# Products of the block inverse as 64x64 tiles, and half of the recurrence's matmuls on the array's other diagonal

## The chip, the cores and the metric

The kernel runs on one core of one Trainium2 chip. The metric is the device time of the whole program in microseconds (us), the median of three runs.

## The reference, cut to what matters here

The program is two transformer-like blocks over 512 tokens of width 1024. The change lies in the first block's mixer, an RWKV recurrence of 8 heads of 64 channels, run over 256 context tokens and then 512 tokens, forwards (d = 0) and backwards (d = 1):

```python
def wkv_scan(state0, r, decay, kk, b, v, k, reverse):
    def step(S, inp):
        r_t, w_t, kk_t, b_t, v_t, k_t = inp
        sa = jnp.einsum("bhvk,bhk->bhv", S, kk_t)
        S = (S * w_t[:, :, None, :] - sa[..., None] * b_t[:, :, None, :]
             + v_t[..., None] * k_t[:, :, None, :])
        return S, jnp.einsum("bhvk,bhk->bhv", S, r_t)
    ...
```

The kernel does this chunk by chunk: 12 chunks of 64 tokens in each direction, for a pair of heads at a time. Within a chunk the steps become a triangular system, so for each chunk, direction and head the inverse of a 64x64 unit triangular matrix is wanted.

## The kernel before

The 128 partitions hold two heads of 64; there are four such pairs, j = 0 to 3. `prep(j)` makes a pair's operands and `stage(j)` runs its recurrence. `build` calls `proj` (the projections, and `prep(0)` and most of `prep(1)` within it), then `rwkv`, then `tail` (output projection, FFN and the whole second block).

`prep(j)` is a generator. For each direction d it makes decays and gates (names `sg`, `cs`, `ta`, `b`), the operands `KB` and `KR`, and then the products that the inverse needs (line 633, PSUM tile `pa`, in the tag `mm` with one buffer). A product of two 64-token operands is wanted as four 32x32 blocks: the two on the block diagonal go to `AKD`, the two beside it to `AKO`. Each block is one matmul of 64 rows and 32 columns of the array, so a direction has 12 chunks x 2 blocks x 2 heads = 48 of them for `AKD` and 48 for `AKO`. One ACT copy (line 188) takes each set out of PSUM. `AKD` has one buffer, `AKO` two.

`inverse(j)` then works on both directions at once. DVE transposes `AKD` into `U` (line 662) and inverts all 32x32 diagonal blocks by 31 steps of two DVE operations on `tmp` and `X` (lines 670, 671), and transposes `X` into `F1` and `F2` (lines 673, 674, both `F` in the rows). PE multiplies `AKO` by them in 32x32 tiles (`pt`, line 691), ACT copies (`T`), PE multiplies again (`po`, lines 698 and 699), and ACT writes the last blocks of the result `XT`.

`stage(j)` runs 12 groups g; in each group one chunk of either direction. For two groups at a time, `pair` makes scores (`psc`, masked by DVE into `AS`, line 731) and transposed operands (`pkt`, copied by ACT into `kbt`). A chunk's chain is: residual `pr` (from `AS`, `vt` and from `KR`, the state `S`), ACT copy to `RU`, correction `pu` (`XT` times `RU`), ACT copy, state update `p3` (`kbt`, `RU`), ACT copy to `S`; and an output `py` beside it. `pr`, `pu` and `py` lie in one PSUM bank for each direction, `p3` in another. All these matmuls go through `mmh`: one matmul for each head, rows 64h to 64h+63 of the array into columns 64h to 64h+63. After a stage, `gn(j)` normalises its output (`ys`, `gm`, `yc`, `gv`), the last stage's on the way to the output projection.

A scheduler sets the order of the work on each engine, by priorities: a stage takes 200 for each group, and the steps of `prep` (a step ends at each `yield`) are taken up between, 4 in each group of stage 0, 2 in stage 1. Stages 0 and 1 so carry `prep(2)` and `prep(3)`. The buffers of `prep` are given up when `inverse(3)` is done; their room goes to the weights of what follows, first to the 32 loads `adaw` with one DVE product each (line 540, `ada12`), which run beside stages 2 and 3.

Of the kernel before, what the change touches and what calls it, by code (L numbers as in the profile page):

```python
# [10 lines left out]
F32 = mybir.dt.float32  # L11
# [7 lines left out]
P = 128  # L19
# [103 lines left out]
class K:  # L123
# [120 lines left out]
    def build(self):  # L244
        tc = self.tc
        with ExitStack() as es:
            self.dr = es.enter_context(tc.tile_pool(name="dr", bufs=1, space=bass.MemoryType.DRAM))
            self.ea = es.enter_context(ExitStack())
            p0 = self.p0 = self.pool(es, "p0", side="left")
            self.cst = p0.tile([P, NCST], F32, name="cst")  # L250
            self.vec = p0.tile([P, NVEC], F32, name="vec")
            self.mod = p0.tile([P, 48, 2], F32, name="mod")
            self.scz = p0.tile([P, KD, 32], F32, name="scz")
            self.mhalf = p0.tile([P, 16], F32, name="mhalf")
            zxb = p0.tile([P, KD, NX], F32, name="zx")
            self.zx = [zxb[:, k, :] for k in range(KD)]
            with ExitStack() as er:
                r0 = self.r0 = self.pool(er, "r0", side="left")
                self.sg = r0.tile([P, NX], F32, name="sg")
                self.vD = self.dr.tile([P, 4, 12, 64], F32, name="vD")  # L260
                self.rD, self.kD, self.kkD = [[self.dr.tile([P, n], F32, name=f"{t}D{j}") for j in range(4)] for t, n in (("r", NX), ("k", NT), ("kk", NT))]
                st = lambda p, name, shape: p.tile([P] + shape, F32, name=name)
                XT0, XT1 = self.XT0, _ = st(r0, "XT0", [24, 64]), zxb[:, 5:8, :].rearrange("p a (b c) -> p (a b) c", c=64)
                set0 = {"KB": [st(r0, f"KB0{d}", [12, 2, 64]) for d in range(2)], "KR": [st(r0, f"KR0{d}", [1280]) for d in range(2)]}
                self.sets = [dict(set0, XT=XT0), {"XT": XT1}, None, dict(set0, XT=XT0)]
                self.hb, self.kah = st(r0, "hb", [16]), st(r0, "kah", [4, 4])
                with ExitStack() as ep:
                    self.pp = self.pool(ep, "pp", side="right")
                    self.lin = [self.pp.tile([P, NT], F32R, name=f"lin{i}") for i in range(2)]

                    room = [(f"KB1{d}", 6) for d in range(2)] + [("KR10", 5)]
                    self.room = []
                    for tag, n in room:
                        t = self.pp.tile([P, n, NC_], F32, tag=tag, name="adaw", bufs=1).rearrange("p a b -> p (a b)")
                        self.room += [t[:, i * 512:i * 512 + 512].unsqueeze(1) for i in range(n // 2)]
                    self.psp = self.psum(ep, "psp", side="right")
                    self.AKD = st(self.pp, "AKD", [32, 32])
                    with ExitStack() as e1:
                        self.wp = self.r1 = self.pool(e1, "r1", side="left")
# [19 lines left out]
    def proj(self):  # L299
# [48 lines left out]
        for kc in range(KD):  # L348
# [4 lines left out]
            for i in range(2):  # L353
# [5 lines left out]
                    nc.gpsimd.tensor_tensor(out=hlo[i][kc], in0=xT[i][kc], in1=hhi[i][kc].bitcast(F32), op=ALU.subtract)  # L359
                else:  # L360
                    nc.vector.scalar_tensor_tensor(out=hlo[i][kc], in0=xT[i][kc], scalar=sh, in1=hhi[i][kc].bitcast(F32), op0=ALU.add, op1=ALU.subtract)
        nc.gpsimd.memset(self.AKD, 0.0)

        def tile_of(u, x=True, c=True):
            ws = [ahead.pop((u, k0), None) or piece(u, k0) for k0 in (0, 4)]
# [179 lines left out]
    def prep(self, j):  # L545
# [23 lines left out]
        nc.scalar.activation(out=bo, in_=pb, func=AF.Copy)  # L569
        S["bo"] = bo  # L570
        ch = lambda t: t.rearrange("p (c t) -> p c t", t=64)
        AKO = S["AKO"] = pp.tile([P, 24, 32], F32, tag="AKO", name="AKO", bufs=2)
        for d in range(2):
            def lora(i, out, bias):

# [46 lines left out]
            nc.vector.tensor_tensor(out=krx[:, :, 1, :], in0=ch(rt), in1=inc[:, 4:12, :], op=ALU.mult)  # L622
            yield

            for off, A in enumerate((self.AKD, AKO)):
                pa = psm(384, "pa")
                for c in range(12):
                    kp = krc[:, c, :] if c < 4 else krx[:, c - 4, 0, :]
                    lt, rt_ = (kp, kb[:, c, bs, :]) if d else (kb[:, c, bs, :], kp)
                    for q in range(2):  # L630
                        o, i = 32 * q, 32 * (q ^ off)
                        for h in (0, 64):
                            nc.tensor.matmul(pa[h + o:h + o + 32, c * 32:c * 32 + 32], lt[h:h + 64, o:o + 32], rt_[h:h + 64, i:i + 32], start=True, stop=True)
                    if c == 5:
                        yield
                self.copy(nc.scalar, A[:, 12 * d:12 * d + 12, :], pa.rearrange("p (c t) -> p c t", t=32))
                yield
        yield from self.inverse(j)

    def mmh(self, out, lt, rt, start=True, stop=True):  # L640

        for h in range(2):
            hs = slice(64 * h, 64 * h + 64)
            self.nc.tensor.matmul(out[hs], lt[hs], rt[hs], start=start, stop=stop)

    @contextmanager
    def prio(self, p):
# [6 lines left out]
    def inverse(self, j):  # L654
# [2 lines left out]

        nc, pp = self.nc, self.pp
        big = lambda name: pp.tile([P, 32, 32], F32, tag="inv", name=name, bufs=3)
        XT, AKO = self.S[j]["XT"], self.S[j]["AKO"]  # L660
        U, tmp, X = big("U"), big("tmp").rearrange("p a b -> p (a b)"), big("X")
        nc.vector.transpose(out=U, in_=self.AKD.rearrange("p n i -> p i n"))
        nc.gpsimd.memset(X, 0.0)
        nc.gpsimd.memset(X.rearrange("p a b -> p (a b)")[:, ::33], 1.0)
        for k in range(31):
# [7 lines left out]
        nc.vector.transpose(out=F1.rearrange("p n i -> p i n"), in_=X)  # L673
        nc.vector.transpose(out=F2.rearrange("p n j -> p j n"), in_=X.rearrange("p i j -> p j i"))
        yield
        b0, b1 = [slice(o, o + 32) for o in (0, 64)], [slice(o + 32, o + 64) for o in (0, 64)]
        D = slice(0, 12), slice(12, 24)
        for r, F in zip(D, (F1, F2)):
            self.copy(nc.vector, XT[:, r, :].rearrange("p n (q i) -> p n q i", q=2), F[:, r, :].unsqueeze(2).to_broadcast([P, 12, 2, 32]))
# [6 lines left out]
        for r in D:  # L686
            yield
            pt = ps("pt")
            for n in range(r.start, r.stop):
                for h in range(2):  # L690
                    nc.tensor.matmul(pt[b1[h], n - r.start, :], AKO[b0[h], n, :], F2[b0[h], n, :], start=True, stop=True)
            for h in range(2):
                self.copy(nc.scalar, T[b1[h], r, :], pt[b1[h]])
        yield
# [9 lines left out]
    def stage(self, j, S, todo, rb, gn):  # L704
# [35 lines left out]
        for g in range(12):  # L740
            at = base + self.PK * g
            with self.prio(at):
                if g % 2 == 0:
                    for d in range(2):
                        pair(g // 2, d)
                for d in range(2):
                    c = chunk(d, g)
                    A, kt, KR, x = cells.pop((d, c))
                    V, S0 = vt[:, c, :], self.S0[d]
                    R, U = (self.RU[d][g % 2][:, i, :] for i in range(2))  # L750
                    pr, pu, py = (self.C1[d][:, i * 64:i * 64 + 64] for i in range(3))
                    p3 = self.C2[d][:, 0:64]
                    self.mmh(pr, A[:, 0:64], V, True, g == 0)
                    if g:
                        self.mmh(pr, KR[:, 0:64], S0, False, True)
                    nc.scalar.activation(out=R, in_=pr, func=AF.Copy)
                    if g < 11:
                        self.mmh(p3, kt[:, 0], V, True, False)
                        if g:
                            self.mmh(p3, id2, S0, False, False)  # L760
                    self.mmh(pu, XT[:, 12 * d + c, :], R)
                    nc.scalar.activation(out=U, in_=pu, func=AF.Copy, scale=-1.0)
                    if x:
                        self.mmh(py, A[:, 64:P], V, True, False)
                        self.mmh(py, KR[:, 64:P], S0, False, False)
                    if g < 11:
                        self.mmh(p3, kt[:, 1], U, False, True)
                        nc.scalar.activation(out=S0, in_=p3, func=AF.Copy, scale=S["PC"][d][:, c:c + 1])
                    if x:
                        self.mmh(py, A[:, P:192], U, False, True)  # L770
                        self.copy(nc.scalar, Y[d][:, c - 4, :], py)
            with self.prio(at + self.PG):
                next(gn, None)
# [6 lines left out]
    def gn(self, j, Y, bo, vt):  # L780
# [43 lines left out]
        yield  # L824
        py = self.ps2.tile([P, 8, 64], F32, tag="sc", name="py", bufs=2)
        for i in range(8):
            self.mmh(py[:, i, :], yc[:, i, :], self.c("id2"))
        nc.vector.scalar_tensor_tensor(out=z, in0=py.rearrange("p a b -> p (a b)"), scalar=self.v("lng", j), in1=z, op0=ALU.mult, op1=ALU.add)
        yield
        if j < 3:  # L830
# [564 lines left out]
```

## Time and profile before

| | |
|---|---|
| median of three runs | 1617.11 us (1615.75 to 1618.56) |
| the profiled execution | 1620.11 us, of which its span is 1618.3 us |
| TensorE (PE), busy | 1533.4 us, 95% |
| VectorE (DVE), busy | 998.3 us, 62% |
| ScalarE (ACT), busy | 629.8 us, 39% |
| stages 0 to 3 | from about 260 to 552 us in the span |

Busy time of PE counts a matmul to the end that the profile models for it, so a row of small matmuls that wait for one another's results can still read as busy. The table of 40 slices is in steps of 40.5 us. [...]

### The profile page before, as it was taken

What the parts mean: (1) busy time and instruction counts of PE and PEld (TensorE: products, weight loads), DVE (VectorE), ACT (ScalarE), POOL (GpSimd) and SP (SyncE); (2) the same over time, 40 slices, a digit from 0 to 9 for tenths busy, and PEclk for the clock granted to TensorE, in tenths of its full rate; (3) what the DMA queues carried; (4) which work ended last, traced back from release to release, by engine and by line L of the source; (5) the groups of instructions that cost most, each with busy time, mean ns of one, the idle gap of its engine ahead of it and who ended that gap; (6) DMA issues with size and microseconds to landing.
All of it is one profiled execution on the core that took longest, in us unless ns stands there. A gap on an engine that the chain in (4) does not pass through costs nothing. (4 is left out here: it accounts for less than half of the span.)

```text
span 1618.3 us, 31205 instructions
## 1 busy us (share of the span) xinstructions
PE 1533.4 (95%) x13214; PEld 1254.0 (77%) x13214; DVE 998.3 (62%) x1689; ACT 629.8 (39%) x1258; POOL 116.8 (7%) x133
## 2 busy tenths in 40 slices
PE   4999999899988899999999997999999999999998
PEld 2877777788777699888888885887677888888886
DVE  3447758873577478888883437678965555554221
ACT  3524344454244344333332335334554333333222
POOL 1111000110101000000000004121200000000000
PEclk9999999797689999999999999999999999999999
DMA  9243321100138442323223332211022222323321
GB/s 333 85 155 101 105 85 57 35 13 4 38 108 258 152 142 80 104 91 104 92 89 94 95 101 69 90 56 51 27 66 91 92 91 91 103 93 92 104 82 61
DMA packets 62188, 152.98 MB, mean 95 GB/s; under 512 B 12640, under 2 KB 14432, under 8 KB 62048
## 3 DMA queue, kind: packets, MB, share of 16 engines
q1 hardware_dynamic: 58016, 143.95, 27.6%
q10 hardware_dynamic: 4032, 7.04, 1.3%
q8 instruction: 103, 1.69, 0.4%
q14 instruction: 37, 0.30, 0.1%
HBM read 143.10 MB, written 7.86 MB: 93 GB/s over the span
## 5 line engine op out<-in xcount | busy, mean ns | idle before, releaser
L181 ACT ACTIVATE whi<-w 128x1024 fp32r<-128x1024 f32 (+2 forms) x220 | 209.0, 952 | 453.6 <-PE pm L170 336.2
L182 DVE TENSOR_TENSOR wlo<-w,whi 128x1024 fp32r<-128x1024 f32 (+2 forms) x212 | 229.5, 1084 | 211.5 <-ACT whi L181 206.8
L169 PE MATMUL pm<-ahi,whi 128*128 128x512 f32 (+1 forms) x624 | 236.5, 379 | 2.6 <-DVE sh L1078 2.2
L170 PE MATMUL pm<-alo,whi 128*128 128x512 f32 (+1 forms) x624 | 234.8, 376 | 0.0
L171 PE MATMUL pm<-ahi,wlo 128*128 128x512 f32 (+1 forms) x624 | 234.0, 375 | 0.0
L170 PE MATMUL pm<-al,whi 128*128 128x512 f32 x352 | 139.7, 397 | 0.0
L169 PE MATMUL pm<-ah,whi 128*128 128x512 f32 x352 | 139.2, 395 | 0.0
L171 PE MATMUL pm<-ah,wlo 128*128 128x512 f32 x352 | 139.2, 395 | 0.0
L169 PEld LDWEIGHTS pm<-ahi,whi 128*128 128x128 f32 x624 | 117.6, 188 | 23.9 <-ACT sh L1093 2.6
L171 PEld LDWEIGHTS pm<-ahi,wlo 128*128 128x128 f32 x624 | 117.6, 188 | 20.9 <-issue 0.7
L170 PEld LDWEIGHTS pm<-alo,whi 128*128 128x128 f32 x624 | 117.6, 189 | 20.0 <-issue 0.7
L951 DVE SCALAR_TENSOR_TENSOR cv<-pm,vec,cv 128x441 f32<-128x441 f32 (+2 forms) x176 | 121.1, 693 | 4.1
L171 PEld LDWEIGHTS pm<-ah,wlo 128*128 128x128 f32 x352 | 66.2, 188 | 16.1 <-issue 0.2
L170 PEld LDWEIGHTS pm<-al,whi 128*128 128x128 f32 x352 | 66.2, 188 | 16.1 <-issue 0.2
L169 PEld LDWEIGHTS pm<-ah,whi 128*128 128x128 f32 x352 | 66.2, 188 | 16.0
L169 PE MATMUL pm<-hhi,whi 128*128 128x512 f32 x176 | 71.3, 405 | 0.5 <-ACT whi L181 0.5
L171 PE MATMUL pm<-hhi,wlo 128*128 128x512 f32 x176 | 70.6, 401 | 1.0 <-DVE wlo L182 1.0
L170 PE MATMUL pm<-hlo,whi 128*128 128x512 f32 x176 | 69.9, 397 | 0.0
L169 PE MATMUL pd<-whi,gh 128*128 128x512 f32 x176 | 69.5, 395 | 0.0
L169 PE MATMUL pm<-hh,whi 128*128 128x512 f32 x176 | 69.3, 394 | 0.0
L170 PE MATMUL pm<-hl,whi 128*128 128x512 f32 x176 | 69.3, 394 | 0.0
L171 PE MATMUL pm<-hh,wlo 128*128 128x512 f32 x176 | 69.3, 394 | 0.0
(397 smaller groups left out, 3140.2 us busy)
## 6 DMA issues: line engine op xcount, KB each, us to landing
w<-in_fup SPq DMA_DIRECT2D x44, 512.0 KB, 3.4
adaw<-in_adat SPq DMA_DIRECT2D x32, 512.0 KB, 4.6
w<-in_win SPq DMA_DIRECT2D x44, 256.0 KB, 2.9
w<-in_wg SPq DMA_DIRECT2D x22, 512.0 KB, 3.4
w<-in_wu SPq DMA_DIRECT2D x22, 512.0 KB, 3.4
w<-in_wd SPq DMA_DIRECT2D x22, 512.0 KB, 3.6
w<-in_win SPq DMA_DIRECT2D x18, 512.0 KB, 3.4
w<-in_wout SPq DMA_DIRECT2D x16, 512.0 KB, 3.8
```

Of the source, the lines that this page charges most:

```text
L169: nc.tensor.matmul(out, lh, rh, start=(first and i == 0), stop=False)
L170: nc.tensor.matmul(out, lh, rl, start=False, stop=False)
L171: nc.tensor.matmul(out, ll, rh, start=False, stop=(last and i == n - 1))
L181: self.nc.scalar.activation(out=hi, in_=src, func=AF.Copy)
L182: (eng or self.nc.vector).tensor_tensor(out=lo, in0=src, in1=hi.bitcast(F32), op=ALU.subtract)
L951: nc.vector.scalar_tensor_tensor(out=o, in0=p[:, ro[0] + dr:ro[1] + dr, co[0] + dc:co[1] + dc], scalar=w(i), in1=o, op0=ALU.mult, op1=ALU.add)
```

## The change

The products of the inverse are made as whole 64x64 blocks, one matmul for each chunk and head, in two sets of six chunks for each direction; they land in one tile `AK` of 24 x 64 columns with one buffer, which takes the place of `AKD` and `AKO`. Before the inverse, two GpSimd (POOL) copies bring the second diagonal block beside the first; a `yield` follows them. `mmh` gets a switch, `swap`: head h then goes from rows 64h into the columns of the other head. It is set for `pa`, `pr`, `pu`, `py` and for the transposition of `yc` in `gn`, so that the two heads stand exchanged in `AK`, `XT`, `RU`'s first half and `Y`, and come back into place in the second product. `p3`, `psc`, `pkt` stay as they were.

```diff
-                    self.AKD = st(self.pp, "AKD", [32, 32])
+                    self.AK = st(self.pp, "AK", [32, 64])
...
-        AKO = S["AKO"] = pp.tile([P, 24, 32], F32, tag="AKO", name="AKO", bufs=2)
...
-            for off, A in enumerate((self.AKD, AKO)):
+            for q in range(2):
                 pa = psm(384, "pa")
-                for c in range(12):
+                for c in range(6 * q, 6 * q + 6):
                     kp = krc[:, c, :] if c < 4 else krx[:, c - 4, 0, :]
                     lt, rt_ = (kp, kb[:, c, bs, :]) if d else (kb[:, c, bs, :], kp)
-                    for q in range(2):
-                        o, i = 32 * q, 32 * (q ^ off)
-                        for h in (0, 64):
-                            nc.tensor.matmul(pa[h + o:h + o + 32, c * 32:c * 32 + 32], lt[h:h + 64, o:o + 32], rt_[h:h + 64, i:i + 32], start=True, stop=True)
-                    if c == 5:
-                        yield
-                self.copy(nc.scalar, A[:, 12 * d:12 * d + 12, :], pa.rearrange("p (c t) -> p c t", t=32))
+                    self.mmh(pa[:, (c - 6 * q) * 64:(c - 6 * q) * 64 + 64], lt, rt_, swap=True)
+                n = 12 * d + 6 * q
+                self.copy(nc.scalar, self.AK[:, n:n + 6, :], pa.rearrange("p (c t) -> p c t", t=64))
                 yield
...
-            hs = slice(64 * h, 64 * h + 64)
-            self.nc.tensor.matmul(out[hs], lt[hs], rt[hs], start=start, stop=stop)
+            hs, ho = (slice(64 * i, 64 * i + 64) for i in (h, h ^ swap))
+            self.nc.tensor.matmul(out[ho], lt[hs], rt[hs], start=start, stop=stop)
...
+        for h in range(2):
+            nc.gpsimd.tensor_copy(out=AK[b1[h], 0:24, 0:32], in_=AK[b1[h], 0:24, 32:64])
+        yield
         U, tmp, X = big("U"), big("tmp").rearrange("p a b -> p (a b)"), big("X")
-        nc.vector.transpose(out=U, in_=self.AKD.rearrange("p n i -> p i n"))
+        nc.vector.transpose(out=U, in_=AK[:, :, 0:32].rearrange("p n i -> p i n"))
...
-                    self.mmh(pr, A[:, 0:64], V, True, g == 0)
+                    self.mmh(pr, A[:, 0:64], V, True, g == 0, swap=True)
                     if g:
-                        self.mmh(pr, KR[:, 0:64], S0, False, True)
+                        self.mmh(pr, KR[:, 0:64], S0, False, True, swap=True)
...
-                    self.mmh(pu, XT[:, 12 * d + c, :], R)
+                    self.mmh(pu, XT[:, 12 * d + c, :], R, swap=True)
...
-                        self.mmh(py, A[:, P:192], U, False, True)
+                        self.mmh(py, A[:, P:192], U, False, True, swap=True)
```

What the scheduler makes of it is seen in three places. First PE near the end of stage 1, where the products of `prep(3)`, d = 1, are made. `pkt` and `psc` are the operands and scores of the stage's next two groups, `c` the PSUM tiles of the chain. (The shapes are those of the moving operand; a 32x32 row of `pa` has 64 rows of the array.) Before, where one row stands for the other for some 40 rows:

```order
L644 MATMUL pkt<-cst,KB_1789 64x64
L633 MATMUL pa<-KB_85,KR_87 32x32
L644 MATMUL pkt<-cst,KB_1789 64x64
L633 MATMUL pa<-KB_85,KR_87 32x32
L644 MATMUL pkt<-cst,KB_1789 64x64
L633 MATMUL pa<-KB_85,KR_87 32x32 x2
L644 MATMUL psc<-KR_1792,KB_1790 64x128
L633 MATMUL pa<-KB_85,KR_87 32x32
```

and PE at the same products in the changed kernel, which make up these three rows and none besides:

```order
L639 MATMUL pkt<-cst,KB_2360 64x64 x8
L639 MATMUL pa<-KB_85,KR_87 64x64 x8
L639 MATMUL c_2375<-RU_2369,zx 64x64 x2
L639 MATMUL pa<-KB_85,KR_87 64x64 x4
L639 MATMUL c_2376<-RU_2371,zx 64x64 x2
L639 MATMUL c_2375<-vt,AS_2366 64x64 x2
L639 MATMUL c_2375<-S_2373,KR_1648 64x64 x2
L639 MATMUL c_2377<-RU_2369,kbt 64x64 x2
L639 MATMUL c_2375<-RU_2369,AS_2366 64x64
L639 MATMUL pa<-KB_85,KR_87 64x64 x12
```

The 96 matmuls in single file with the stage's are now 24 in three pieces. From the first score of stage 0 to the end of the recurrence `pa` stands in 74 rows on PE before and in 13 now; the neighbours in PE's row that lie on different diagonals are 479 now and none before. Second, ACT in stage 0, at the end of `inverse(1)`; `T` are its copies, `zx` its results, `AK` (`AKD`, `AKO`) the products of `prep(2)`. Before:

```order
L188 ACTIVATE T<-pt 32x384 x4
L188 ACTIVATE zx<-po 32x12x32 x4
L188 ACTIVATE AKD<-pa 128x384
L188 ACTIVATE kbt<-pkt 128x256
L756 ACTIVATE RU_2633<-c_2639 128x64
```

and ACT at the same end of `inverse(1)` in the changed kernel:

```order
L188 ACTIVATE AK<-pa 128x384
L188 ACTIVATE T<-pt 32x384 x2
L762 ACTIVATE RU_2370<-c_2375 128x64
L188 ACTIVATE T<-pt 32x384 x2
L188 ACTIVATE AK<-pa 128x384
L768 ACTIVATE S_2373<-c_2377,pc 128x64
```

Before, the `AKD` shown is that of d = 1; the products of d = 0 had left PSUM 27 and 26 rows above the first row shown. Now those of d = 0 stand among the copies of `inverse(1)`, since its `pt` still reads `AK`, and what follows in `prep(2)` stands behind them. Third, DVE from the end of `inverse(1)` to the start of `inverse(2)`. Before, where these twelve rows are all there is between:

```order
L673 STREAM_TRANSPOSE F_2869<-X 128x32x32
L674 STREAM_TRANSPOSE F_2870<-X 128x32x32
L192 COPY zx<-F_2869 128x768
L192 COPY zx<-F_2870 128x768
L613 SCALAR_TENSOR_TENSOR KB_2625<-b_3428,sg 128x12x64
L621 TENSOR_TENSOR KR_2627<-kk,cs 128x8x64
L615 TENSOR_TENSOR b_3428<-ta,kt 128x768
L622 TENSOR_TENSOR KR_2627<-rt,cs 128x8x64
L616 TENSOR_TENSOR KB_2625<-b_3428,sg 128x12x64
L731 COPY_PREDICATED AS_2629<-cst,psc 128x384
L731 COPY_PREDICATED AS_2631<-cst,psc 128x384
L662 STREAM_TRANSPOSE U<-AKD 128x1024
```

and DVE from the same place in the changed kernel, where `U` comes three rows after the last one shown:

```order
L192 COPY zx<-F_2520 128x768
L730 COPY_PREDICATED AS_2366<-cst,psc 128x384
L190 TENSOR_SCALAR sg<-sg,cst 128x12x64
L594 SCALAR_TENSOR_TENSOR cs<-cst,sg 128x780
L730 COPY_PREDICATED AS_2368<-cst,psc 128x384
L611 SCALAR_TENSOR_TENSOR b_2983<-ta,kk 128x768
L730 COPY_PREDICATED AS_2365<-cst,psc 128x2x64
L612 SCALAR_TENSOR_TENSOR KB_2361<-b_2983,sg 128x12x64
L619 TENSOR_TENSOR KR_2363<-kk,cs 128x256
L620 TENSOR_TENSOR KR_2363<-kk,cs 128x8x64
L614 TENSOR_TENSOR b_2983<-ta,kt 128x768
L621 TENSOR_TENSOR KR_2363<-rt,cs 128x8x64
```

Now the whole of d = 1 (`sg`, `cs`, `b`, `KB`, `KR`) comes after the end of `inverse(1)`, where before only its last half did. Counted in masks `AS` of the stages (12 in each) ahead of them in DVE's row, the three ends `F` of inverses 1 to 3 stood behind 8, 18 and 30, and stand behind 10, 22 and 32 now.

## Rows read from the trace of the kernel before

**Rows 1.** The page: busy time of the engines, and the granted clock in 40 slices.

```profile
PE 1533.4 (95%) x13214; PEld 1254.0 (77%) x13214; DVE 998.3 (62%) x1689; ACT 629.8 (39%) x1258; POOL 116.8 (7%) x133
...
PEclk9999999797689999999999999999999999999999
```

**Rows 2.** Stretches: us, then busy us (instructions) of PE, PEld, DVE, ACT, POOL, PEclk.

```profile
260.00:300.00 40.00, 37.55 (x977) 31.39 (x968) 34.48 (x82) 21.52 (x75) 0.57 (x2) 1.00 0.03 9
...
380.00:430.00 50.00, 49.33 (x851) 39.63 (x852) 21.13 (x42) 17.16 (x63) 1.51 (x4) 0.74 0.01 4
...
470.00:550.00 80.00, 68.26 (x1611) 59.19 (x1606) 56.94 (x98) 35.19 (x149) 4.90 (x3) 1.00 0.75 240
```

**Rows 3.** Timeline of PE, stage 1: start, us, operation, number of passes merged.

```profile
409.06 0.31 PE L633 MATMUL pa<-KB,KR 64*32 64x32 f32 x2
409.30 0.47 PE L644 MATMUL pkt<-cst,KB 64*64 64x64 f32 x2
409.70 0.31 PE L633 MATMUL pa<-KB,KR 64*32 64x32 f32 x2
```

**Rows 4.** Timeline of PE, stage 1, some 47 us earlier.

```profile
361.95 0.24 PE L633 MATMUL pa<-KR,KB 64*32 64x32 f32 x2
362.12 0.32 PE L644 MATMUL c<-vt,kbt 64*64 64x64 f32 x2
362.38 0.24 PE L633 MATMUL pa<-KR,KB 64*32 64x32 f32 x2
```

**Rows 5.** Timeline of PE, stage 3, matmuls of one tile size alone.

```profile
522.58 0.28 PE L644 MATMUL c<-S,KR 64*64 64x64 f32 x4
522.70 0.28 PE L644 MATMUL c<-RU,kbt 64*64 64x64 f32 x4
```

**Rows 6.** DVE, starts of `U` and `F`: inverses 1 to 3, idle time before in brackets.

```profile
301.77 1.95 DVE L673 STREAM_TRANSPOSE F<-X 128x1024 f32<-128x1024 f32 x1
...
315.45 1.95 DVE L662 STREAM_TRANSPOSE U<-AKD 128x1024 f32<-128x1024 f32 x1 [4.32 <-ACT AKD L188]
...
361.33 1.92 DVE L673 STREAM_TRANSPOSE F<-X 128x1024 f32<-128x1024 f32 x1
...
403.60 1.93 DVE L662 STREAM_TRANSPOSE U<-AKD 128x1024 f32<-128x1024 f32 x1 [8.13 <-ACT AKD L188]
...
451.88 1.95 DVE L673 STREAM_TRANSPOSE F<-X 128x1024 f32<-128x1024 f32 x1
```

**Rows 7.** Waits of DVE, 315.5 to 361.3: us in total, times, longest.

```profile
DVE AS L731 <- PE psc L644: 7.7, 3, 5.3
```

**Rows 8.** The same, 361.4 to 403.7.

```profile
DVE AS L731 <- PE psc L644: 11.7, 2, 11.2
DVE U L662 <- ACT AKD L188: 8.1, 1, 8.1
DVE sg L190 <- ACT sg L580: 3.6, 1, 3.6
```

**Rows 9.** The same, 403.7 to 451.9.

```profile
DVE AS L731 <- PE psc L644: 16.3, 6, 9.2
```

**Rows 10.** POOL's groups by form: a plain copy of 64 partitions x 512.

```profile
L1127 POOL COPY kz<-ak 64x512 f32<-64x512 f32 x4 | 3.5, 878 | 13.7 <-ACT ak L1119 13.6
```

**Rows 11.** Timeline of POOL and DVE: `gn` of stages 2 and 3 begins with `ys`.

```profile
493.17 2.25 POOL L807 TENSOR_TENSOR ys<-Y 128x512 f32<-128x512 f32 x1
...
552.12 1.14 DVE L807 TENSOR_TENSOR ys<-Y 128x512 f32<-128x512 f32 x1 [6.60 <-ACT Y L188]
```

**Rows 12.** Tile `adaw`: durations ns min/median/max, first and last start in us.

```profile
L540 DVE SCALAR_TENSOR_TENSOR adaw<-adaw,cb x32: 1208/1224/1939, 471.3 to 533.8; 128x1024 f32<-128x1024 f32 x32
```

**Rows 13.** Timeline, PE and its weight loads (PEld), `po` of `inverse(0)`.

```profile
189.66 0.21 PE L698 MATMUL po<-F,T 32*32 32x32 f32 x1
189.67 0.10 PEld L699 LDWEIGHTS po<-T,F 32*32 32x32 f32 x1
```

**Rows 14.** Tile `S`: weight loads and matmuls of `S` times the identity, ns min/median/max.

```profile
L644 PEld LDWEIGHTS c<-S,cst x320: 129/135/228, 266.0 to 545.9; 64*64 64x64 f32 x160
```

More of the change, by code (lines that the diff above doesn't have):

```diff
@@ L361, in proj @@
                     nc.vector.scalar_tensor_tensor(out=hlo[i][kc], in0=xT[i][kc], scalar=sh, in1=hhi[i][kc].bitcast(F32), op0=ALU.add, op1=ALU.subtract)
-        nc.gpsimd.memset(self.AKD, 0.0)
+        nc.gpsimd.memset(self.AK, 0.0)
         def tile_of(u, x=True, c=True):
@@ L623, in prep, with mmh @@
             yield
-            for off, A in enumerate((self.AKD, AKO)):
+            for q in range(2):
                 pa = psm(384, "pa")
-                for c in range(12):
+                for c in range(6 * q, 6 * q + 6):
                     kp = krc[:, c, :] if c < 4 else krx[:, c - 4, 0, :]
                     lt, rt_ = (kp, kb[:, c, bs, :]) if d else (kb[:, c, bs, :], kp)
-                    for q in range(2):
-                        o, i = 32 * q, 32 * (q ^ off)
-                        for h in (0, 64):
-                            nc.tensor.matmul(pa[h + o:h + o + 32, c * 32:c * 32 + 32], lt[h:h + 64, o:o + 32], rt_[h:h + 64, i:i + 32], start=True, stop=True)
-                    if c == 5:
-                        yield
-                self.copy(nc.scalar, A[:, 12 * d:12 * d + 12, :], pa.rearrange("p (c t) -> p c t", t=32))
+                    self.mmh(pa[:, (c - 6 * q) * 64:(c - 6 * q) * 64 + 64], lt, rt_, swap=True)
+                n = 12 * d + 6 * q
+                self.copy(nc.scalar, self.AK[:, n:n + 6, :], pa.rearrange("p (c t) -> p c t", t=64))
                 yield
         yield from self.inverse(j)
-    def mmh(self, out, lt, rt, start=True, stop=True):
+    def mmh(self, out, lt, rt, start=True, stop=True, swap=False):
         for h in range(2):
-            hs = slice(64 * h, 64 * h + 64)
-            self.nc.tensor.matmul(out[hs], lt[hs], rt[hs], start=start, stop=stop)
+            hs, ho = (slice(64 * i, 64 * i + 64) for i in (h, h ^ swap))
+            self.nc.tensor.matmul(out[ho], lt[hs], rt[hs], start=start, stop=stop)
     @contextmanager
@@ L659, in inverse @@
         big = lambda name: pp.tile([P, 32, 32], F32, tag="inv", name=name, bufs=3)
-        XT, AKO = self.S[j]["XT"], self.S[j]["AKO"]
+        XT, AK = self.S[j]["XT"], self.AK
+        b0, b1 = [slice(o, o + 32) for o in (0, 64)], [slice(o + 32, o + 64) for o in (0, 64)]
+        for h in range(2):
+            nc.gpsimd.tensor_copy(out=AK[b1[h], 0:24, 0:32], in_=AK[b1[h], 0:24, 32:64])
+        yield
         U, tmp, X = big("U"), big("tmp").rearrange("p a b -> p (a b)"), big("X")
-        nc.vector.transpose(out=U, in_=self.AKD.rearrange("p n i -> p i n"))
+        nc.vector.transpose(out=U, in_=AK[:, :, 0:32].rearrange("p n i -> p i n"))
         nc.gpsimd.memset(X, 0.0)
@@ L675, in inverse @@
         yield
-        b0, b1 = [slice(o, o + 32) for o in (0, 64)], [slice(o + 32, o + 64) for o in (0, 64)]
         D = slice(0, 12), slice(12, 24)
@@ L690, in inverse @@
                 for h in range(2):
-                    nc.tensor.matmul(pt[b1[h], n - r.start, :], AKO[b0[h], n, :], F2[b0[h], n, :], start=True, stop=True)
+                    nc.tensor.matmul(pt[b1[h], n - r.start, :], AK[b0[h], n, 32:64], F2[b0[h], n, :], start=True, stop=True)
             for h in range(2):
@@ L760, in stage @@
                             self.mmh(p3, id2, S0, False, False)
-                    self.mmh(pu, XT[:, 12 * d + c, :], R)
+                    self.mmh(pu, XT[:, 12 * d + c, :], R, swap=True)
                     nc.scalar.activation(out=U, in_=pu, func=AF.Copy, scale=-1.0)
                     if x:
-                        self.mmh(py, A[:, 64:P], V, True, False)
-                        self.mmh(py, KR[:, 64:P], S0, False, False)
+                        self.mmh(py, A[:, 64:P], V, True, False, swap=True)
+                        self.mmh(py, KR[:, 64:P], S0, False, False, swap=True)
                     if g < 11:
@@ L826, in gn @@
         for i in range(8):
-            self.mmh(py[:, i, :], yc[:, i, :], self.c("id2"))
+            self.mmh(py[:, i, :], yc[:, i, :], self.c("id2"), swap=True)
         nc.vector.scalar_tensor_tensor(out=z, in0=py.rearrange("p a b -> p (a b)"), scalar=self.v("lng", j), in1=z, op0=ALU.mult, op1=ALU.add)
```

## The prediction

> **What bounds the kernel now.** I read the page first, then the stretches, then the timeline of PE and DVE's waits. PE is busy 95% of the span [rows 1], so at first sight whatever shortens PE's work pays. But the change only touches what lies before about 552 us, and there PE's busy time hides two different things. From 260 to 300 us DVE works 34.5 of 40 us: it paces that stretch. From 380 to 430 DVE works 21.1 of 50 us and PE reads 49.3 of 50 [rows 2]. That stretch is PE's, though it holds fewer PE instructions (851 in 50 us) than the first (977 in 40 us).
>
> The timeline shows why. Where a `pa` matmul (64x32 tile) and a stage's matmul (64x64) take turns, one of each takes 0.64 us (409.06 to 409.70), at the lower clock [rows 3, 1], and 0.43 us (361.95 to 362.38) at the full one [rows 4]. Where all matmuls have the 64x64 tile, two of them (four passes) take 0.12 us [rows 5], so one of each would be some 0.1 us. The rest is the change of tile size, twice: PE's next start comes only after the matmul in flight has all but drained. The other engines stand behind this: DVE's starts of the inverse (`U`) waited 4.3 and 8.1 us for `AKD` [rows 6], and its masks `AS` waited for `psc` 7.7, 11.7 and 16.3 us in the three stretches from 315 to 452 us [rows 7 to 9]. So between 315 and 452 us the bound is PE's order, and the way out of it is the chain of the inverses on DVE: `F` of `inverse(3)` ends at 451.9, and only then do the `adaw` loads of the next phase get their buffers.
>
> After 452 us another limit shows: 32 `adaw` products start from 471.3 to 533.8 [rows 12], 2.0 us apart, against 1.2 us that one takes, while the DMA engines run at 0.75 and 240 GB/s [rows 2]. That phase is paced by its loads.
>
> **The change part by part.** All sums are against the profiled execution: 1620.1 us, 3.0 above the median of the runs shown; I move the median by the same gain.
>
> The products. 96 matmuls of a direction become 24, and their tile size is that of their neighbours. What they cost by themselves is small both ways: 24 matmuls at 0.06 us are 1.4 us [rows 5]. What goes is the taking turns, and with it the waits of DVE on PE. I follow the chain of `U` and `F` [rows 6]:
>
> - `F` of `inverse(1)`, at 301.8 before: its `U` now waits for both sets of products, the second some 0.7 us of PE and an ACT copy, and for two POOL copies of 24x32 = 768 elements in a partition. The nearest row is a POOL copy of 512 in 0.88 us [rows 10], so 1.3 us each, 2.6 for both; with two more masks ahead of `F` I take 5 us. Behind `U` on DVE stand the inverse's steps and the next masks, for which PE's chain waits. Later by 5: 307.
> - `F` to `U` of `inverse(2)`: 13.7 us before. This gets longer. `AK` has one buffer, the products of `prep(2)` stand among the copies of `inverse(1)`, and the whole of d = 1 comes behind `F`; on ACT the copy to `AK` that waits for `pt` has the chain's copies to `RU` and `S` behind it, but PE, at `pt`, holds the chain there too. The like of that is the next such interval before, 361.3 to 403.6, which had the same DVE work in it: 42.3 us, of which 11.7 + 8.1 + 3.6 [rows 8] are waits; 18.9 us are left. To that I add 5 us for what can't be hidden (products, ACT, POOL). 24 us: later by 10.
> - `U` to `F` of `inverse(2)`: 45.9 us less the 7.7 of [rows 7], or 38: earlier by 7, rounded down.
> - `F` to `U` of `inverse(3)`: 42.3 before, 24 now: earlier by 18.
> - `U` to `F` of `inverse(3)`: 48.3 less 16.3 [rows 9], 32: earlier by 16.
>
> Together -5 - 10 + 7 + 18 + 16 = 26: `F` of `inverse(3)` at about 426 us. As bounds: if the hops cost nothing and all waits go, 10 more; if half of the 41 us in the last three terms stay, because `pt`, `po` and `pl` still change the tile size there, 20 less.
>
> From `F` of `inverse(3)` to `ys` of stage 3: 552.1 - 451.9 = 100.2 us. Two things must fit. The recurrence has 16 of its 48 masks to go instead of 18, eight pairs of groups; stage 3 took 58.9 us for six [rows 11], 9.8 each, so 78 us. The loads: the first `adaw` came 19.4 us after `F`, the 32 take 64 us, and in the changed order the last of them and three weight splits stand ahead of `ys`; each split needs a load at that pace and an ACT copy, some 8 us for the three as an estimate: 91 us. The larger holds: earlier by 9. If the first `adaw` comes 8 us after `F`, it is 20.
>
> The other diagonal. It can let two matmuls run side by side where four passes now queue on two tiles. The trace has the like of it: two 32x32 matmuls that share rows 32 to 63 and differ in columns start within 10 ns of each other [rows 13]. In the stages the chain is short of nothing of PE's for long once the turns are gone, and from 452 us the loads pace, so I count 0 for it; in stages 0 and 1 the cover is DVE (86% busy from 260 to 300, rows 2). Without that cover, two of the chain's matmuls saved in each of 24 groups in those stages, at 0.06 us for either direction, are some 6 us. They stand in the low end.
>
> The rest. The two POOL copies and the `yield` are in the sum; POOL has 117 us of work in the whole span [rows 1]. In `proj` six sets of products shrink beside projections that fill PE, and `inverse(0)` starts some 4 us later with stage 0 far off: 0, give or take 2. `gn`'s exchange costs nothing: the same 16 matmuls.
>
> Sum: 26 + 9 = 35 us. 1620.1 - 35 = 1585 for the profiled execution, and 1582 for the median.
>
> **The rivals.**
>
> First, the single `AK` takes most of it back. If what I called waits on the turns is in part `pt`, `po` and `pl` holding PE's order (the 11.2 us wait [rows 8] ends among them), and the serial `prep` exposes more than 5 us, the two `F`-to-`U` intervals are 33 us and not 24: 18 us less, 1600. For it: the order, which puts `prep(2)` behind `inverse(1)`, and `F` behind two to four more masks. Against it: pieces of `pa` lie in all three stretches in which DVE waited. At 42 us each nothing is left: 1617 to 1618, the same.
>
> Second, slower: a change of diagonal is not free. In the new order 479 neighbours lie on different diagonals. If each had to wait for its weights, 0.135 us [rows 14], that is 65 us on PE; 1617 + 65 - 35 = 1647 if all lay on the path. It decides from 35 of 65, 54% on the path. Against it: the weight load of the second matmul in [rows 13] starts while the first, on the same rows, is in flight. No 64x64 tiles on both diagonals are in this trace. [...]
>
> Third, more: the two diagonals run together and PE's part of the chain halves in all stages, the first `adaw` comes at once, and the waits all go: 35 + 10 + 11 + 6 = 62, 1555.
>
> That the change doesn't do what it says is part of the first: the exchange may bring no time at all, and the forecast rests on the tile size alone.
>
> **How the numbers follow.** The forecast, a gain of 25 to 50 us, gets 0.6. The first rival gets 0.2 for a gain of 4 to 25 and 0.05 for no change. More than 50 gets 0.07. Slower gets 0.08: 0.06 the second rival, 0.02 DVE's queue held at `U` by a late POOL copy with the masks behind it. Faster by over 0.2% (3.2 us, about what a measurement of this kernel can tell from no change): 0.6 + 0.2 + 0.07 = 0.87; same 0.05; slower 0.08. The range: 20 us less and 4 more from the first rival give 1606; all bounds of the terms but the hops, 21 + 35 = 56 less, 1561. Beyond 1606 lie 0.05 + 0.08 and a little of the first rival, beyond 1561 some 0.05.
>
> **What would show it.** Right: no idle or slow turns of `pa` from 315 to 425, `U` of `inverse(3)` near 394 and `F` near 426, `adaw` 2.0 us apart as before, `ys` of stage 3 near 517, all after that shifted whole. Wrong: `F` to `U` over 33 us (first rival); starts of PE 0.13 us apart where diagonals alternate (second). What I leave out: the clock. It was at its lower level for part of 300 to 470 us [rows 1]; if it stays up there, more is won, if it falls after 470, where it was full [rows 2], some is lost.

## The result, and the profile after

The changed kernel takes 1593.4 us (1592.3 to 1595.3), the kernel before 1616.4: a ratio of 0.985 (0.983 to 0.987). Timed again beside the last experiments it gave 0.981 (0.979 to 0.984). The gain is 23 to 31 us, within the range of the prediction (1561 to 1606) and 11 us short of its 1582. The profiled execution took 1594.2 us, its span 1592.4.

The page of the kernel after, busy time and granted clock, the lines that answer to [rows 1]:

```profile
PE 1490.4 (94%) x12062; PEld 1214.2 (76%) x12062; DVE 999.6 (63%) x1689; ACT 629.5 (40%) x1258; POOL 123.9 (8%) x141
...
PEclk9999999778779999999999998999999999999999
```

DVE's starts of `U` and `F` after the change, from its timeline (start, us, operation, idle time before and its releaser), as in [rows 6]:

```profile
262.48 1.97 DVE L662 STREAM_TRANSPOSE U<-AK 128x1024 f32<-128x1024 f32 x1 [0.71 <-POOL AK L659]
...
297.54 1.96 DVE L673 STREAM_TRANSPOSE F<-X 128x1024 f32<-128x1024 f32 x1
...
326.38 1.96 DVE L662 STREAM_TRANSPOSE U<-AK 128x1024 f32<-128x1024 f32 x1 [2.75 <-POOL AK L659]
...
371.82 1.93 DVE L673 STREAM_TRANSPOSE F<-X 128x1024 f32<-128x1024 f32 x1
...
397.06 1.96 DVE L662 STREAM_TRANSPOSE U<-AK 128x1024 f32<-128x1024 f32 x1 [0.19 <-POOL AK L659]
...
432.76 1.96 DVE L673 STREAM_TRANSPOSE F<-X 128x1024 f32<-128x1024 f32 x1
```

The stretches between them (us, then busy us (instructions) of PE, PEld, DVE, ACT, POOL, then PEclk):

```profile
297.50:326.40 28.90, 26.17 (x610) 22.05 (x612) 13.60 (x19) 16.31 (x49) 3.94 (x8) 0.65 0.13 43
326.40:371.80 45.40, 38.56 (x874) 31.32 (x870) 38.46 (x89) 20.87 (x78) 7.33 (x8) 0.81 0.05 16
371.80:397.10 25.30, 22.37 (x615) 18.45 (x611) 13.74 (x19) 16.63 (x51) 3.94 (x8) 0.87 0.02 4
397.10:432.80 35.70, 29.90 (x722) 25.47 (x718) 29.11 (x77) 14.76 (x65) 4.97 (x5) 0.76 0.05 14
432.80:523.50 90.70, 68.90 (x1754) 57.64 (x1753) 65.06 (x109) 41.55 (x155) 7.73 (x8) 0.84 0.69 219
```

`F` of `inverse(3)` ends the chain of inverses 19.1 us earlier than before (432.8 against 451.9), `ys` of stage 3 comes 28.6 us earlier (523.5 against 552.1), and the span is 25.9 us shorter. The tiles `ys` and `adaw` (durations in ns, first and last start), as in [rows 11, 12]:

```profile
L807 DVE TENSOR_TENSOR ys<-Y x1: 1285/1285/1285, 523.5 to 523.5; 128x512 f32<-128x512 f32 x1
```

```profile
L540 DVE SCALAR_TENSOR_TENSOR adaw<-adaw,cb x32: 1203/1224/1852, 451.7 to 515.3; 128x1024 f32<-128x1024 f32 x32
```

The turns of [rows 3, 4] are gone. In the PE rows of the trace between 200 and 500 us, runs of `pa` passes fell from 77 to 30, and the time from start to start at the borders of these runs from 28.4 to 5.4 us in all. (A matmul of these stands in the trace as two passes: the 768 of the kernel before as 1536. There are more runs here than the 13 rows of the order, since these 300 us begin ahead of stage 0 and passes of neighbouring matmuls stand between one another.)

### The profile page after: what moved, and what is told of

Same layout as the page of the kernel before. It is cut to its first block, busy times and chain, and to the rows that moved or that the text cites. A ratio compares the mean times of both kernels' runs of the same rounds, so it can differ in the third digit from the quotient of the medians.

```text
span 1592.4 us, 28924 instructions
## 1 busy us (share of the span) xinstructions
PE 1490.4 (94%) x12062; PEld 1214.2 (76%) x12062; DVE 999.6 (63%) x1689; ACT 629.5 (40%) x1258; POOL 123.9 (8%) x141
## 5 line engine op out<-in xcount | busy, mean ns | idle before, releaser
L170 PE MATMUL pd<-wlo,gh 128*128 128x512 f32 x176 | 69.2, 393 | 0.0
```

The costliest lines, as they stand in the source:

```text
L170: nc.tensor.matmul(out, lh, rl, start=False, stop=False)
```

## The experiments

Twelve kernels ran. Each was timed against the kernel before on its own chip, so the ratios are what to compare. `U(j)` and `F(j)` are the starts of these operations in `inverse(j)` (of `F` the first), `ys(j)` the start of `gn` after stage j, all in us of the profiled execution.

| kernel | median us | ratio to before, 95% | `F(3)` | `ys(1)` | `ys(3)` |
|---|---|---|---|---|---|
| before | 1616 to 1620 | 1 | 451.9 | 430.7 | 552.1 |
| after | 1593.4 | 0.983 to 0.987 | 432.8 | 399.2 | 523.5 |
| after, again | 1589.5 | 0.979 to 0.984 | 428.0 | 395.3 | 518.1 |
| after, one diagonal | 1590.9 | 0.980 to 0.985 | 432.7 | 400.6 | 518.8 |
| before, exchange alone | 1627.2 | 1.004 to 1.008 | 462.6 | 441.1 | 561.0 |
| after, narrow tiles | 1586.7 | 0.979 to 0.983 | 426.8 | 396.8 | 517.2 |
| before, products in lumps | 1584.7 | 0.977 to 0.983 | 421.8 | 402.3 | 522.4 |
| after, two buffers | 1577.0 | 0.973 to 0.977 | 405.1 | 386.4 | 506.8 |
| two buffers, one diagonal | 1575.3 | 0.970 to 0.975 | 407.7 | 389.3 | 507.6 |

**Does the other diagonal do anything?** The changed kernel without the exchange, everything on one diagonal:

```diff
-self.mmh(pa[...], lt, rt_, swap=True)
+self.mmh(pa[...], lt, rt_)
 (and so in pr, pu, py of the stages and py of gn)
```

> The changed kernel with the exchange of heads taken out again: the products of the inverse stay 64x64 tiles, every matmul of the recurrence lies on one diagonal of the array. Theory (the gain of 24 us is the end of the turns between 64x32 and 64x64 tiles, the diagonal counts 0): 1593 us, give or take 3, so the same as the changed kernel; F of inverse(3) near 433 us in the profile. Rival, the second diagonal carries part of the gain: 1598 to 1612, and F(3) later than 436. Rival, each change of diagonal costs a weight load: this kernel is the faster one, 1585 or less.

It took 1590.9 us, ratio 0.983 (0.980 to 0.985): the same as the changed kernel. The other way round, the kernel before with the exchange alone:

```diff
-pa[h + o:h + o + 32, ...]
+pa[64 - h + o:64 - h + o + 32, ...]
 (pr, pu, py and gn's py as in the change; products stay 64x32)
```

> The kernel before with the exchange alone: heads exchanged in AKD, AKO, XT and RU, residuals, corrections and outputs on the other diagonal, products of the inverse still 64x32 tiles. Theory (tile size alone): 1616 us, give or take 3, turns of 0.43 to 0.64 us as in the kernel before. Rival, the second diagonal gives time by itself: 1604 to 1612. Rival, a change of diagonal costs a weight load of 0.135 us: slower than 1620, up to 1680 if every one of the some 480 changes lay on the path.

1627.2 us, 0.55% slower (0.35 to 0.76). The theory missed. The time lies in the wide range of the last rival, but the some 10 us lost are far from the 65 that a weight load at each change of diagonal would cost. Its `pa` passes stand in 89 runs instead of 77, and the borders take 34.2 us instead of 28.4, at a lower clock: 0.79 granted from 200 to 520 us against 0.88 before. So more and somewhat dearer turns make up to 5.8 of the 10.7 us by which `F(3)` is later. What the rest is, the lower clock or the exchange itself, was not separated.

**Is it the tile size?** The changed kernel with only the tile size put back:

```diff
-self.mmh(pa[...64 columns], lt, rt_, swap=True)
+for o in (0, 32):
+    for h in (0, 64):
+        nc.tensor.matmul(pa[64 - h + o:64 - h + o + 32, ...64 columns], lt[h:h + 64, o:o + 32], rt_[h:h + 64], ...)
```

> The changed kernel with only the tile size put back: each 64x64 product as two 64x32 tiles with 64 columns of data each, in the same PSUM tile, with the same copies, the same AK and the exchange kept; 48 matmuls a direction in place of 24. Theory (the change of tile size on PE is the cost): turns of 0.4 to 0.6 us come back, AS waits of 7 us and more from 315 to 433 us, total 1604 to 1617. Rival (the gain comes from fewer instructions, fewer copies or the order): 1592 to 1598.

1586.7 us: no slower than the changed kernel. My theory in this form fell. The timeline of PE of this kernel tells why; the narrow products stand in lumps of up to 48 passes:

```profile
347.03 0.28 PE L641 MATMUL pkt<-cst,KB 64*64 64x64 f32 x2
347.24 0.65 PE L631 MATMUL pa<-KR,KB 64*32 64x64 f32 x32
347.94 0.43 PE L641 MATMUL psc<-KR,KB 64*64 64x128 f32 x2
348.30 0.43 PE L631 MATMUL pa<-KR,KB 64*32 64x64 f32 x16
```

There are 18 runs of `pa` in it between 200 and 500 us, and nothing takes turns. So the narrow tile by itself costs nothing that shows, and the order decides how many changes of size there are. I had put into one cause what are two. The next experiment takes the second alone: the kernel before, with the priority number held while a block of products is written out.

```diff
+at = self.tc.cur_priority
 for h in (0, 64):
+    self.tc.cur_priority = at
     nc.tensor.matmul(pa[h + o:h + o + 32, ...], ...)
 (and `at` is read anew after the yield in the middle)
```

> The kernel before with one thing changed: the priority number is held while a block of products of the inverse is written out, so that the 64x32 products stand on PE in 24 lumps in the recurrence in place of 74 (mostly single) ones. Tile size, tiles, copies and heads are those of before. Theory, revised after the run with narrow tiles (1586.7 us without turns): what costs is that tiles of two sizes take turns, not the narrow tile itself. Expected 1587 to 1605, F of inverse(3) 12 to 25 us earlier than before. Rival (the gain of the change comes from fewer products, the wider tile or fewer steps of prep): 1613 to 1619.

1584.7 us, ratio 0.980 (0.977 to 0.983): the whole gain of the change, with 64x32 tiles, `AKD`, `AKO` and one diagonal as before, and a little better than the 1587 to 1605 expected. Its DVE timeline:

```profile
353.40 1.97 DVE L676 STREAM_TRANSPOSE F<-X 128x1024 f32<-128x1024 f32 x1
...
388.19 1.95 DVE L665 STREAM_TRANSPOSE U<-AKD 128x1024 f32<-128x1024 f32 x1 [4.57 <-ACT AKD L188]
...
421.84 1.96 DVE L676 STREAM_TRANSPOSE F<-X 128x1024 f32<-128x1024 f32 x1
```

`F(3)` at 421.8 is 30 us earlier than before. The borders of `pa` runs are 54 instead of 154, and take 9.2 us instead of 28.4. A held number also puts a block as a whole ahead of later work of the stage, so this run alone doesn't tell fewer turns from an earlier place; the next three do.

**What does a turn cost?** Three kernels add the same 96 products to stage 1 of the changed kernel, into an unused part of `pkt`: narrow and in turns, narrow in lumps, and wide in turns. Their results are read by nobody.

```diff
 nc.tensor.matmul(pk[h:h + 64, c, i], ...)           (the pkt matmul; where j == 1)
+nc.tensor.matmul(pt[h:h + 32, q:q + 32], id2[h:h + 64, 0:32], kb[h:h + 64, c0, d, 0:32], ...)
```

> The changed kernel with 96 extra products of no use in stage 1: after each of the 8 pkt matmuls of a pair one 64x32 product with 32 columns into an unused part of the same PSUM tile. Theory: a turn takes 0.43 to 0.64 us where two 64x64 ones would take some 0.1, so 32 to 52 us of PE in stage 1, at least half of it on the path: 1610 to 1645. Rival (turns cost little, the order of before had another fault): 1593 to 1602.

> The same 96 extra 64x32 products, written in lumps of 8 ahead of the 8 pkt matmuls of a pair. Theory: 15 lumps with two changes of size each at some 0.27 us, and 96 products at 0.02 to 0.03: 8 to 11 us of PE, part of it hidden: 1593 to 1603. Rival (the narrow product itself is dear): as with single turns, 1610 or more.

> The same 96 extra products in turns with the pkt matmuls, but as 64x64 tiles, the size of their neighbours, with the same 32 columns. Theory: 96 at 0.06 us or less, 3 to 6 us of PE: 1592 to 1599. Rival (the taking of turns costs whatever the tile, for example by weight loads): 1610 or more.

Narrow in turns: 1622.7 us (ratio 1.004, 1.002 to 1.007), all of the gain gone. Narrow in lumps: 1586.8. Wide in turns: 1589.8 (both 0.982). Narrow in lumps beat its forecast of 1593 to 1603, wide in turns its 1592 to 1599. Narrow turns against wide ones are 33 us for 96, or 0.34 us each. In PE's rows the borders of the extra products take 33.4 us in narrow turns, 6.7 in wide ones and 6.0 in lumps, so 27 of the 33 us are found there. The granted clock was lower too, 0.70 against 0.92 between `U(2)` and `F(2)`; whether the rest comes from that was not separated. PE's timeline with narrow products in turns, once at the full clock (1.00 granted from 341.0 to 341.8 us) and once near the half (0.55 from 343.5 to 344.3):

```profile
341.18 0.24 PE L739 MATMUL pkt<-KB,cst 64*32 64x32 f32 x2
341.35 0.33 PE L736 MATMUL pkt<-cst,KB 64*64 64x64 f32 x2
341.61 0.25 PE L739 MATMUL pkt<-KB,cst 64*32 64x32 f32 x2
...
343.56 0.31 PE L739 MATMUL pkt<-KB,cst 64*32 64x32 f32 x2
343.81 0.47 PE L736 MATMUL pkt<-cst,KB 64*64 64x64 f32 x2
344.20 0.31 PE L739 MATMUL pkt<-KB,cst 64*32 64x32 f32 x2
```

0.43 us for one of each (341.18 to 341.61) and 0.64 (343.56 to 344.20): the numbers of [rows 3, 4] again, made on purpose. The same place with the extra products as 64x64 tiles:

```profile
340.26 0.34 PE L736 MATMUL pkt<-cst,KB 64*64 64x64 f32 x4 [0.91 <-ACT kbt L188]
340.43 0.26 PE L739 MATMUL pkt<-KB,cst 64*64 64x32 f32 x4
340.51 0.33 PE L736 MATMUL pkt<-cst,KB 64*64 64x64 f32 x4
```

Two of each take 0.25 us, so one of each 0.12. Between the two sizes each start comes 0.06 to 0.08 us before the end of the matmul ahead of it, here 0.17 to 0.18 us before. And the masks wait for `psc` as in [rows 7 to 9]; the largest of DVE's waits from 327.7 to 391.2 with narrow turns (us in total, times, longest), a stretch, `U(2)` to `F(2)`, that takes 63.5 us here and 42.0 with wide ones, where no wait of `AS` for `psc` stands:

```profile
DVE AS L732 <- PE psc L639: 12.8, 4, 5.5
```

**What does the single `AK` cost?** The changed kernel with the blocks of the diagonal in one tile, read early by `U`, and those beside it in a tile with two buffers, read late by `pt`:

```diff
-self.copy(nc.scalar, self.AK[:, n:n + 6, :], pa...)
+for A, o in ((self.AKD, 0), (AKO, 32)):
+    self.copy(nc.scalar, A[:, n:n + 6, :], pa...[:, :, o:o + 32])
```

> The changed kernel with the products in two tiles: the diagonal blocks in one 32x32 tile (read early, by the transposition to U), the blocks beside the diagonal in a tile with two buffers (read late, by pt); four ACT copies of 192 elements in place of two of 384 in each direction. Theory: the single AK costs what the forecast of F to U missed, 28.9 us measured against 24: F(1) to U(2) 24 to 27 us, total 1586 to 1591. Rival one (the single AK took most of the gain back): F(1) to U(2) and F(2) to U(3) both shorter by 5 to 9, total 1575 to 1584. Rival two (the buffer was not the limit, but DVE and the lower clock): 1592 to 1596.

1577.0 us, ratio 0.975 (0.973 to 0.977): faster than the changed kernel by 0.6 to 1%, 10 to 16 us. The time is that of rival one, though the intervals it named shrank far more than it said. In the changed kernel ACT shows how `prep(2)` and `inverse(1)` hold each other up (timeline of ACT):

```profile
302.01 0.49 ACT L188 ACTIVATE AK<-pa 128x384 f32<-128x384 f32 x1 [1.66 <-PE pt L690]
302.52 0.98 ACT L188 ACTIVATE T<-pt 32x384 f32<-32x384 f32 x2
...
306.11 0.49 ACT L188 ACTIVATE AK<-pa 128x384 f32<-128x384 f32 x1
...
309.81 0.47 ACT L579 ACTIVATE sg<-pl,hb 128x256 f32<-128x256 f32 x1
```

The copy of direction 0 waits until `pt` has read the old `AK`, after `F(1)` at 297.5; with it the only PSUM tile of `prep` stays taken, so `sg` of direction 1 starts at 309.8, and the serial work up to `U(2)` lies bare. With two buffers all of this stands ahead of `F(1)`, which is at 304.7:

```profile
281.47 0.33 ACT L188 ACTIVATE AKO<-pa 128x192 f32<-128x192 f32 x1
282.39 0.47 ACT L580 ACTIVATE sg<-pl,hb 128x256 f32<-128x256 f32 x1 [0.48 <-PE pl L579]
...
295.61 0.33 ACT L188 ACTIVATE AKO<-pa 128x192 f32<-128x192 f32 x1
```

Its `F` and `U` on DVE:

```profile
304.73 1.94 DVE L675 STREAM_TRANSPOSE F<-X 128x1024 f32<-128x1024 f32 x1
...
312.90 1.95 DVE L664 STREAM_TRANSPOSE U<-AKD 128x1024 f32<-128x1024 f32 x1 [1.31 <-PE pt L692]
...
361.60 1.96 DVE L675 STREAM_TRANSPOSE F<-X 128x1024 f32<-128x1024 f32 x1
...
369.15 1.95 DVE L664 STREAM_TRANSPOSE U<-AKD 128x1024 f32<-128x1024 f32 x1 [1.35 <-PE pt L692]
...
405.06 1.96 DVE L675 STREAM_TRANSPOSE F<-X 128x1024 f32<-128x1024 f32 x1
```

`F` to `U` takes 8.2 and 7.5 us where it took 28.9 and 25.3; the work moved between `U` and `F` (43.3 and 48.7 against 35.1 and 45.4), and `F(3)` is 27.7 us earlier.

**The best version.** Two buffers with the exchange taken out:

> The kernel with two buffers (1577.0 us) with the exchange of heads taken out: products and recurrence on one diagonal. Theory, after the first four runs: the second diagonal shortens PE's work but not the chain, and the granted clock falls lower for it (0.78 against 0.86 from 300 to 400 us with and without it), so it is worth 0 or costs 1 to 4 us: 1573 to 1577. Rival (with the turns and the single AK out of the way, PE's part of the chain counts and the second diagonal gives time): 1580 to 1590.

1575.3 us, ratio 0.972 (0.970 to 0.975): as fast as with the exchange or a little faster, the fastest of all, and faster than both kernels of this case.

**The clock.** Two runs asked whether PE's idle time costs granted clock. 384 more products of no use in all four stages of the changed kernel, and the changed kernel again beside them:

> The changed kernel with 384 extra products of no use, 64x64 tiles of 32 columns, one after each pkt matmul, in all four stages. They are 15 to 25 us of PE. Theory (PE has room in the recurrence, and what it idles there it pays in granted clock): mean granted clock from 300 to 520 us above the 0.80 of the changed kernel, total 1586 to 1594, no slower than the changed kernel. Rival (the clock is not set by what PE does, and PE's order is the chain): 1597 to 1612, at the same clock.

> The changed kernel itself, beside the other two on the same chip, for differences of a few us. All theories: 1590 to 1596 us.

1595.8 against 1589.5 us (ratios 0.983 to 0.988 and 0.979 to 0.984), and 0.90 granted from 200 to 520 us in both. The extra work did not raise the clock, and it cost 6 us: the theory isn't borne out, and the time lies between it and its rival. The changed kernel itself came out just under the 1590 to 1596 expected; between its two profiles the granted clock of this stretch was 0.86 and 0.90.

**A miss.** The lumps of the kernel before, with two of the four steps that the products of a direction take in `prep` removed:

```diff
-                    if c == 5:
-                        yield
```

> The kernel before with the products in lumps (1584.7 us) and two of the four steps that the products of a direction take in prep removed (the yield in the middle of each set), so that prep has the number of steps of the changed kernel; one diagonal, 64x32 tiles, two buffers for the blocks beside the diagonal, no POOL copies. Theory: what separates the lumps (F(2) to U(3) 34.8 us) from the two buffers on one diagonal (8.2 us, 1575.3) is the number of steps, not tile or copies: F(2) to U(3) 8 to 20 us, total 1570 to 1579. Rival (tile size and the number of products still count): as the lumps, 1581 to 1589.

1588.5 us (0.979 to 0.983): no better than the lumps, and `F(2)` to `U(3)` stays at 36.0 us. DVE's waits there:

```profile
DVE sg L190 <- ACT sg L580: 9.5, 1, 9.5
DVE AS L731 <- PE psc L644: 6.1, 3, 4.8
DVE U L662 <- ACT AKD L188: 3.5, 1, 3.5
```

Direction 1 of `prep(3)` still comes behind `F(2)`, though its buffers are two. So neither the steps nor the buffers alone bring it ahead of `F`; which part of the order does is open.

## Why the prediction was right, and where it was not

**The bound and the cause.** Right: the turns of two tile sizes held PE, PE held the masks, and these the inverses. Narrow turns added to the changed kernel cost 33 us, and lumps alone give the whole gain. Too narrow in one point: "their tile size is that of their neighbours" was taken for what removes the turns. The run with narrow tiles in lumps shows that the order would have done.

**`F(1)`, forecast 5 us later.** It was 4.2 earlier, 297.5. The cost of the hops was real but small: a POOL copy took 0.8 us, where I had taken 1.3, and `U` waited 0.7 us for POOL's `AK` in `inverse(1)`, 2.8 and 0.2 in the next two. What I left out of this term is that direction 0's copy, held by the single `AK`, moved behind `F(1)`, and with it the first work of direction 1: DVE is busy 32.7 us from `U(1)` to `F(1)` instead of 35.2. The stretch had a few turns too, 1.5 us at the borders of `pa` runs before and 0.1 now. It takes 35.1 us instead of 40.7.

**`F(1)` to `U(2)`, forecast 24 us.** 28.9. The step that failed is "to that I add 5 us for what can't be hidden": the longest wait there is one of the masks,

```profile
310.41 0.58 DVE L730 COPY_PREDICATED AS<-cst,psc 128x384 f32<-128x384 int32 x1 [8.28 <-PE psc L639]
```

8.3 us at the place where `pt`, `po` and the two copies to `AK` follow each other. DVE works 13.6 us in this interval and waits 15.3. I had taken all such waits of [rows 8] for turns. This is the first rival in small. It had the mechanism right: the run with two buffers gives 10 to 16 us back. It had its size wrong, since at 28.9 and 25.3 us the two intervals are not the 33 that it wanted. Part of the miss is spread: in the second profile of the changed kernel this interval is 26.5 us, and the three after it 44.7, 24.4 and 34.8.

**`U(2)` to `F(2)`, forecast 38 us.** 45.4, the largest miss of the sum, and 44.7 in the second profile. The step that failed is "45.9 us less the 7.7". The wait of the masks did shrink, to 2.0 us in all, but DVE's own busy time in the stretch is 38.5 us (35.4 before), so 38 without any wait could not hold. There are eight masks in it in both kernels. What came in are the two `zx` of `gn(0)`, 1.4 us, which had stood behind `F(2)`, at 383.2 and 388.3:

```profile
361.23 0.74 DVE L828 SCALAR_TENSOR_TENSOR zx<-py,vec,zx 128x512 f32<-128x512 f32 x1
...
367.26 0.69 DVE L832 TENSOR_TENSOR zx<-pg,zx 128x512 f32<-128x512 f32 x1 [0.35 <-PE pg L799]
```

Two of the masks are wide instead of narrow (0.5 us), and the 31 steps of the inverse take 23.0 us instead of 21.6. A forecast that takes waits away must add the work that moves into their place.

**`F(2)` to `U(3)` and `U(3)` to `F(3)`, forecast 24 and 32 us.** 25.3 and 35.7: right in kind, some 5 us too good together. The sum to `F(3)` was 26 us, measured 19.1, and 23.9 in the second profile. (Of the low end of the range: the 10, 11 and 6 us of its bounds make 22 without the 5 of the hops, not 21; nothing hangs on that.)

**`F(3)` to `ys`, forecast 91 us.** 90.7, with the first `adaw` 18.9 us after `F` and 2.05 us between starts (451.7 to 515.3), as said. But the reason holds less far than the number, which is in part luck: with two buffers `F(3)` comes 27.7 us earlier than in the changed kernel and `ys(3)` only 16.7, so the same stretch takes 101.7 us. In every kernel of the table stages 2 and 3 together, `ys(1)` to `ys(3)`, take 118 to 124 us (121.4 before, 124.3 after, 120.4 with two buffers), and 113 to 126 in the five others. The better mark for this kernel is `ys(1)`, the end of stage 1: it moved by 31.5 us in the changed kernel and by 44.3 with two buffers, and the spans by 25.9 and 43.5.

**The other diagonal, counted 0.** Right in both kernels without turns. The second rival, a weight load at each change of diagonal, fell. The timeline of the changed kernel at 450 us, PE and its weight loads (PEld), where 0.50 of the clock was granted:

```profile
450.65 0.37 PE L639 MATMUL c<-vt,AS 64*64 64x64 f32 x2
450.68 0.18 PEld L639 LDWEIGHTS c<-RU,kbt 64*64 64x64 f32 x2
450.68 0.37 PE L639 MATMUL c<-RU,kbt 64*64 64x64 f32 x2
...
450.81 0.32 PE L639 MATMUL c<-vt,AS 64*64 64x64 f32 x2
...
450.84 0.32 PE L639 MATMUL c<-RU,kbt 64*64 64x64 f32 x2
450.91 0.42 PE L639 MATMUL c<-S,KR 64*64 64x64 f32 x4
...
451.12 0.32 PE L639 MATMUL c<-RU,AS 64*64 64x64 f32 x2
```

A product on the exchanged diagonal (`vt,AS`) and one on the other (`RU,kbt`), of both heads, start 0.03 us apart and repeat after 0.16 us. These eight passes take 0.26 us (450.65 to 450.91) where the four of `S,KR`, all on one diagonal, take 0.21 (450.91 to 451.12), so the two diagonals run side by side in part. The weights of `RU,kbt` go to the same rows as those of `vt,AS`, whose first passes run from 450.65 to 451.02; their load starts at 450.68, so it didn't wait for these to end. The second rival's price is not seen in the times either: 1590.9 us on one diagonal, 1589.5 to 1593.4 on both.

**The clock, left out.** In the kernel before, 0.50 of it was granted at the turns of [rows 3] (409.0 to 409.8 us) and 1.00 at those of [rows 4] (361.9 to 362.4). After the change, from 432.8 to 523.5 us 0.84 of it was granted, where from 470 us on it had been full [rows 2]; yet that stretch took what was forecast. Of the 28.6 us at `ys` 2.7 are gone by the end of the span. From `ys(3)` to the end takes 1065 to 1070 us in the profiled kernels (1066.2 before, 1068.9 and 1065.2 in two profiles of the changed kernel), so these 2.7 us are within the spread.

## What to carry to other kernels

Count the changes of tile size on PE, not the small tiles: here 0.34 us each time a single narrow product slipped between wide ones, and nothing that shows for a lump (1586.8 us with the 96 in lumps, 1589.8 with wide ones in turns). A scheduler that orders by priority numbers makes such turns unseen; holding one number for a block, three lines, was worth as much here as the whole rewrite. When two uses of a tile are merged into one, look at which of its readers is the last: the late reader `pt` held up the next pair's early writer, for 10 to 16 us.

## What the runs showed of the hardware that was not expected

With two diagonals side by side PE's busy time was shorter and the granted clock lower, in each of three pairs. From 200 to 520 us, without and with the exchange:

| pair | PE busy us | granted clock | ratio to before |
|---|---|---|---|
| products as before | 298.6, 287.7 | 0.88, 0.79 | 1, 1.0055 |
| products of the change | 291.2, 269.0 to 274.2 | 0.94, 0.86 to 0.90 | 0.983, 0.981 to 0.985 |
| two buffers | 294.5, 275.8 | 0.97, 0.89 | 0.972, 0.975 |

The rows of the last pair, two buffers on one diagonal,

```profile
200.00:520.00 320.00, 294.49 (x5844) 250.17 (x5842) 236.06 (x457) 158.94 (x529) 43.79 (x54) 0.97 0.29 95
```

and with both:

```profile
200.00:520.00 320.00, 275.75 (x5833) 226.95 (x5831) 233.40 (x453) 157.00 (x529) 36.83 (x54) 0.89 0.29 95
```

PE does the same products in less busy time and is granted less clock, and the kernel gains nothing: the time stays in two pairs and is 0.55% longer in the first. The granted clock over the whole span says the same in every execution: 0.945 to 0.956 against 0.959 to 0.972 in the first pair, 0.955 to 0.968 against 0.971 to 0.979 in the second, 0.962 to 0.969 against 0.979 to 0.985 in the third, with the exchange the lower each time. That less work causes the lower clock was not shown: the run with extra products left the clock where it was.
